# A decoder trunk on one core: squares taken off the output projections, memory tokens in smaller pieces, matmuls issued long pair then short pair

## The chip, the core and the metric

The kernel runs on one core of a Trainium2 chip. The metric is the device time of one execution in microseconds (us). A core has several engines that run at the same time, each with its own queue of instructions in order: TensorE (PE; its weight loads are listed apart as PEld), VectorE (DVE), ScalarE (ACT), GpSimd (POOL) and SyncE (SP), which issues the DMA transfers here. SBUF is the on-chip memory, PSUM the memory that matmuls accumulate in.

## The reference

One layer of a decoder with 256 positions and a width of 2048, in float32, then a final RMS norm:

```python
h = rms_norm(x, norm_mix[l])
z = h @ w_in[l]
...
x = x + jnp.concatenate([out_a, out_b, out_c], axis=-1) @ w_out[l]
h = rms_norm(x, norm_xattn[l])
m = rms_norm(mem, norm_mem[l])
q = (h @ xattn_wq[l]).reshape(bsz, S, X_HEADS, HEAD_DIM)
kv = (m @ xattn_wkv[l]).reshape(bsz, n_mem, 2, X_HEADS, HEAD_DIM)
...
x = x + o @ xattn_wo[l]
h = rms_norm(x, norm_mlp[l])
x = x + jnp.square(jax.nn.relu(h @ w_up[l])) @ w_down[l]
```

out_a is a gated MLP with a layer norm, out_b a dilated attention, out_c a sparse attention; o is a cross attention over 256 memory tokens (mem). Each RMS norm needs the sum of squares of a row of 2048.

## The kernel before

**Precision.** Every large product is made in three parts. An activation or a weight tile is split into a high part (ScalarE copies it to fp32r, L82 or with a gain L87) and a low part (VectorE subtracts the high part from the source, L83 or L88). The product is high x high + low activation x high weight + high activation x low weight. For weights the parts are called wh and wl, the source raw. A weight tile of 512 KB comes by DMA into one of five raw buffers; wh and wl have three buffers each.

**Products with weights on the left.** `gemm_t` makes a product that comes out transposed (features on partitions, positions along the row). It takes four chunks of 512 rows; each chunk is one weight tile, one wh and one wl, and `products_t` issues its 16 matmuls: for each of four row blocks kk and two feature blocks f a long matmul (`main`, 512 columns: high and low activation side by side against wh, L158) and a short one (`low`, 256 columns: high activation against wl, L162). The two f have accumulators in different PSUM banks. `low` goes first except in the first row block of a product. `gemm_t` serves the products k, cq, bk, bq, u, wo (output projection), mk, xq and up; the first product, cmp, calls `products_t` itself. `gemm` (L204, all long: dn, mv, bv, v) and `gemm_t1` (L147, all short: xo) are other helpers.

**Stages.** cmp and k first, then the sparse and the dilated attention, the gating branch (v with a layer norm into zu, then u0 and u1, then the matmuls psv with the gating weights into mix0), eight output projections wo0 to wo7 (each makes 256 of the 2048 features, from the four mix tiles in the order 2, 3, 1, 0), memory keys mk, queries xq, scores, memory values mv, eight products xo, then four times eight products up and four products dn.

**Squares and memory tokens.** After each output projection and each xo, `add_residual` adds the product to the residual xres on VectorE (L565), scales and splits it for the next product (tiles h, L87 and L88), and calls `add_squares`: ScalarE squares (L101), and POOL adds into ssq (L103), or VectorE at the start of the kernel. The memory tokens are loaded, scaled and split (tiles mT) and squared (ssqm) behind the projections wo2 to wo5, 512 KB at a time, through the same five raw buffers. `mean_eps` sums the squares over partitions (half of it on POOL) and TensorE adds them up (pss).

**Order.** The program is written in this order, but the build schedules it against a model of the engines: on each engine the instructions stand in the order that this scheduler chose, which can pull work forward over other work whose inputs come later. What runs is that order, not the text's.

Of the kernel before, what the change touches and what calls it, by code (L numbers as in the profile page):

```python
# [8 lines left out]
F32 = mybir.dt.float32  # L9
F32R = mybir.dt.float32r  # L10
AF = mybir.ActivationFunctionType
ALU = mybir.AluOpType
# [3 lines left out]
P = 128  # L16
S = 256
# [20 lines left out]
def trunk_kernel(ctx: ExitStack, tc: tile.TileContext, a, out):  # L38
# [6 lines left out]
    nc = tc.nc  # L45
# [21 lines left out]
    def slot(tag, name, dtype=F32R):  # L67
        t = ap.tile([P, 4, 2, S], F32R, tag=tag, name=name)
        return t if dtype == F32R else f32(t)
# [6 lines left out]
    def load_raw(src, n=1024):  # L76
        t = wp.tile([P, 1024], F32, tag="raw", bufs=5, name="raw")
        loads.append(nc.sync.dma_start(t[:, :n], src))
        return t[:, :n]
# [5 lines left out]
    def split_scaled(hi, lo, src, g):  # L85

        nc.scalar.activation(hi, src, AF.Copy, scale=g)  # L87
        nc.vector.scalar_tensor_tensor(lo, src, g, f32(hi), op0=ALU.mult, op1=ALU.subtract)  # L88
# [6 lines left out]
            split_scaled(t[:, k % 4, 0, :], t[:, k % 4, 1, :], src[:, i, :], gT[:, gi, k:k + 1])  # L95


    def add_squares(ssq, src, first, add=None):

        sq = ssq if first else sp.tile([P, 2, S], F32, tag="sq", name="sq")  # L100
        nc.scalar.activation(sq, src, AF.Square)  # L101
        if not first:
            (add or nc.gpsimd).tensor_tensor(ssq, ssq, sq, op=ALU.add)  # L103

    def mean_eps(ssq, name):

# [44 lines left out]
    def products_t(acc, x, wh, wl, first, last):  # L151

        for kk in range(4):
            for f in range(2):
                fs = slice(f * P, (f + 1) * P)

                def main(start, stop):
                    nc.tensor.matmul(acc[:, f].rearrange("p a s -> p (a s)"), wh[:, kk, fs],  # L158
                                     x[:, kk].rearrange("p a s -> p (a s)"), start=start, stop=stop)

                def low():
                    nc.tensor.matmul(acc[:, f, 0, :], wl[:, kk, fs], x[:, kk, 0, :], start=False, stop=False)  # L162

                if first and kk == 0:
                    main(True, False)
                    low()
                else:
                    low()
                    main(False, last and kk == 3)

    def gemm_t(lhs, wsrc, name, order=None, between=None):

        acc = pacc.tile([P, 2, 2, S], F32, tag="acc", name=name)
        order = order or list(range(len(lhs)))
        for n, b in enumerate(order):
            wh, wl = (w.rearrange("p (k n) -> p k n", k=4) for w in split_w(load_raw(wsrc[b])))
            products_t(acc, lhs[b], wh, wl, n == 0, n == len(order) - 1)
            if between is not None:
                next(between, None)
        return acc  # L180
# [97 lines left out]
    def squares():  # L278

        for m, acc in enumerate(cmps):  # L280
            join(acc, "cmp", kraw[:, 2 * m:2 * m + 2, :])
        for b in range(4):
            for n in (2 * b, 2 * b + 1):
                add_squares(ssq, xres[:, 2 * n:2 * n + 2, :], n == 0, add=nc.vector)
            yield

    acc_k0 = gemm_t(hx, a["w_t"][KV], "k0", between=squares())
# [249 lines left out]
    nc.vector.tensor_tensor(zv, zv, lng[:, 0:1, :].to_broadcast([P, 2, NB]), op=ALU.mult)  # L537
    nc.vector.tensor_tensor(zv, zv, lng[:, 1:2, :].to_broadcast([P, 2, NB]), op=ALU.add)

    for m in range(2):  # L540
        acc = gemm_t(hx, a["w_t"][UU + m], f"u{m}")
        j = join(acc, "u")
        nc.vector.tensor_tensor(j, j, rxb[:, None, :].to_broadcast([P, 2, S]), op=ALU.mult)
        nc.scalar.activation(uT[:, 2 * m:2 * m + 2, :], j, AF.Gelu_apprx_tanh)
# [14 lines left out]
            split(mix[0][:, g, 0, :], mix[0][:, g, 1, :], uT[:, g, :])  # L559


    def add_residual(acc, parts, n, ssq, act, gi):
        xs = xres[:, 2 * n:2 * n + 2, :]
        for i in range(parts):
            nc.vector.tensor_tensor(xs, acc[:, :, i, :], xs, op=ALU.add)  # L565
        put_act(act, 2 * n, xs, gi)
        add_squares(ssq, xs, n == 0)


    ssq = sp.tile([P, 2, S], F32, tag="ssq", name="ssq2")  # L570
    ssqm = sp.tile([P, 2, S], F32, tag="ssq", name="ssqm")
    h2 = new_act("hA", "h2")
    mT = []
    for n in range(8):
        acc = gemm_t(mix, a["w_out"][n], f"wo{n}", order=[2, 3, 1, 0])
        add_residual(acc, 2, n, ssq, h2, 1)
        if n >= 2 and n < 6:
            j = n - 2
            mT.append(slot("hC", f"mT{j}"))
            raw = load_raw(a["memT"][j]).rearrange("p (k s) -> p k s", k=4)  # L580
            for kk in range(4):
                split_scaled(mT[j][:, kk, 0, :], mT[j][:, kk, 1, :], raw[:, kk, :], gT[:, 2, 4 * j + kk:4 * j + kk + 1])
            for i in range(2):
                add_squares(ssqm, raw[:, 2 * i:2 * i + 2, :], j == 0 and i == 0)
    rm = rstd(mean_eps(ssqm, "mm"), "rm")
    rmb = along_free(rm, "rmb")

# [1 line left out]
    xk, xq = slot("hB", "xk"), slot("hB", "xq")  # L589
    xv = slot("hB", "xv", F32).rearrange("p k a s -> p (k a s)")[:, :1024].rearrange("p (t n) -> p t n", t=2)  # L590
    px = slot("hB", "px", F32)
    for m in range(2):
        acc = gemm_t(mT, a["w_mk"][m], f"mk{m}")
        join_split(acc, xk[:, 2 * m:2 * m + 2, 0, :], xk[:, 2 * m:2 * m + 2, 1, :], "mk", rmb)
    for m in range(2):
        acc = gemm_t(h2, a["w_q"][m], f"xq{m}")
# [26 lines left out]
    for h in range(4):  # L623
# [8 lines left out]
        for mb in range(2):  # L632
            nc.tensor.matmul(o, xv[:, mb, h * HD:(h + 1) * HD], pT[:, mb, :], start=(mb == 0), stop=(mb == 1))
        split(oT[:, h, 0, :], oT[:, h, 1, :], o)
    ssq = sp.tile([P, 2, S], F32, tag="ssq", name="ssq3")
    h3 = new_act("hB", "h3")
    for n in range(8):
        add_residual(gemm_t1(oT, a["w_xo"][n][0], f"xo{n}"), 1, n, ssq, h3, 3)


    gfin = slot("hA", "gfin", F32).rearrange("p k a s -> p (k a s)")
# [4 lines left out]
    for q in range(4):  # L646
        hid = new_act("hC", f"hid{q}")
        for c in range(8):
            acc = gemm_t(h3, a["w_up"][8 * q + c], f"up{q}{c}")
            z = join(acc, "up")  # L650
            nc.vector.scalar_tensor_tensor(z, z, 0.0, z, op0=ALU.max, op1=ALU.mult)  # L651
            ht = hid[c // 2][:, 2 * (c % 2):2 * (c % 2) + 2]
            split(ht[:, :, 0, :], ht[:, :, 1, :], z)
            if q == 0:
                if c == 0:
                    r3 = mean_eps(ssq, "m3")
                    nc.vector.reciprocal(r3, r3)
                t, n = c % 2, c // 2
                ps = pmisc.tile([P, 4, P], F32, tag="tr", name="trx")
                for i in range(4):  # L660
                    nc.tensor.transpose(ps[:, i, :], xres[:, 4 * n + i, t * P:(t + 1) * P], ident)
                nc.scalar.activation(xt[t][:, n * NB:(n + 1) * NB], ps.rearrange("p i s -> p (i s)"), AF.Copy)
        for n in range(4):
            ns = slice(n * NB, (n + 1) * NB)
            final = q == 3 and n == 3
            acc = gemm(hid, a["w_down"][4 * q + n], 2, NB, f"dn{q}{n}", hold=4 if final else 0)
            for t in range(2):
                xs = xt[t][:, ns]
                nc.vector.scalar_tensor_tensor(xs, acc[t], r3[:, t:t + 1], xs, op0=ALU.mult, op1=ALU.add)  # L669
                if q == 3:  # L670
                    j = sp.tile([P, NB], F32, tag="sq", name="sqf")
                    nc.scalar.activation(j, xs, AF.Square, accum_out=ssqf[:, t, n:n + 1])
                    if not final:
                        nc.vector.tensor_tensor(xs, xs, gfin[:, ns], op=ALU.mult)
                if q == 3 and n == 2:

                    nc.vector.tensor_reduce(sf[:, t:t + 1], ssqf[:, t, :3], axis=AX.X, op=ALU.add)
                    nc.vector.tensor_scalar(sf[:, t:t + 1], sf[:, t:t + 1], 1.0 / D, EPS, op0=ALU.mult, op1=ALU.add)  # L678
                if final:
                    s_ = sf[:, t:t + 1]  # L680
                    nc.vector.scalar_tensor_tensor(s_, ssqf[:, t, 3:4], 1.0 / D, s_, op0=ALU.mult, op1=ALU.add)
# [104 lines left out]
```

## Time and profile before

| | |
|---|---|
| median of 3 runs (lowest to highest) | 1205.95 us (1204.63 to 1206.29) |
| the profiled execution's own time | 1206.72 us |
| its span in the trace | 1204.7 us |
| granted TensorE clock, mean | 0.999 |
| longest group of TensorE waits | 4.3 us, at the start |
| DMA | 224.24 MB, 186 GB/s over the span |

The profile is of one execution. Busy time is the time in which an engine runs an instruction; a share says nothing of which engine sets the end. The chain of work follows the last instruction back to what released it, step by step, so its steps on TensorE are the distance from one matmul to the next. The rows of waits give total us, number and longest. Windows give the busy time of every engine between two times. The rows of groups give the busy us and the mean ns of one, and the length of one matmul there holds its latency too, so that neighbours overlap.

### The profile page before, as it was taken

Reading aid. Unit: us, or ns where it says so; the run is one execution under the profiler, and the core shown is the slowest. Engines: PE = TensorE matmul, PEld = TensorE weight load, DVE = VectorE, ACT = ScalarE, POOL = GpSimd, SP = SyncE. Lnnn points to the kernel's source line nnn. Section 1 sums busy time; section 2 is a strip of 40 time slices with the busy share of each in tenths; the row PEclk is TensorE's granted clock in tenths of the full one; section 3 lists DMA queues with packets and bytes.
Section 4 is the critical chain, followed back from the end, with each engine's and each line's share of the span. In section 5 each row is a group of like instructions: output and inputs, shape, how many; then the busy total and the mean of one; then the engine's idle time right before and its main releaser. Section 6 shows DMA issues by size and latency. Waiting matters only on the chain.

```text
span 1204.7 us, 16460 instructions
## 1 busy us (share of the span) xinstructions
PE 1183.8 (98%) x6450; PEld 1018.5 (85%) x6450; DVE 743.3 (62%) x911; ACT 592.2 (49%) x808; POOL 42.9 (4%) x39
## 2 busy tenths in 40 slices
PE   7999999999989999999999999999999999999996
PEld 6898888888878889888888888888888888888885
DVE  7775786666886667756544565545566545556554
ACT  7564555454665466544433444433444333444443
POOL 0000000000123001100000000000000000000000
PEclk9999999999999999999999999999999999999999
DMA  8675434545566554555665555555555555555653
GB/s 288 213 265 184 138 123 136 182 158 181 178 218 202 188 171 163 177 190 188 190 197 193 186 183 192 192 192 193 190 180 190 193 194 193 190 188 181 196 188 105
DMA packets 65385, 224.24 MB, mean 186 GB/s; under 512 B 7963, under 2 KB 9499, under 8 KB 65179
## 3 DMA queue, kind: packets, MB, share of 16 engines
q1 hardware_dynamic: 65307, 223.19, 57.0%
q8 instruction: 50, 0.82, 0.3%
q14 instruction: 28, 0.23, 0.1%
HBM read 221.06 MB, written 2.10 MB: 185 GB/s over the span
## 4 chain that ended last, share of the span: by engine, by line
PE 92%; DVE 3%; DMA 2%; issue 1%; ACT 1%; SPq 0%; ACTq 0%; POOLq 0%; POOL 0%; DVEq 0%
PE dn L204 27%; PE up L158 20%; PE up L162 10%; PE wo L158 3%; PE cq L158 2%; PE xo L147 2%; PE bv L204 2%; PE v L204 2%; PE mv L204 2%; PE wo L162 2%; DVE wl L83 1%; PE cq L162 1%; PE xq L158 1%; PE u L158 1%; PE bk L158 1%
## 5 line engine op out<-in xcount | busy, mean ns | idle before, releaser
L83 DVE TENSOR_TENSOR wl<-raw,wh 128x1024 fp32r<-128x1024 f32 (+3 forms) x414 | 500.6, 1212 | 345.9 <-ACT wh L82 344.1
L82 ACT ACTIVATE wh<-raw 128x1024 fp32r<-128x1024 f32 (+3 forms) x414 | 428.8, 1038 | 445.0 <-PE dn L204 185.5
L158 PE MATMUL up<-h,wh 128*128 128x512 f32 x1024 | 359.3, 398 | 0.0
L204 PE MATMUL dn<-wh,hid 128*128 128x512 f32 x992 | 306.1, 389 | 0.0
L162 PE MATMUL up<-h,wl 128*128 128x256 f32 x1024 | 282.4, 281 | 0.0
L158 PEld LDWEIGHTS up<-h,wh 128*128 128x128 f32 x1024 | 190.6, 188 | 44.2
L204 PEld LDWEIGHTS dn<-wh,hid 128*128 128x128 f32 x992 | 186.2, 188 | 38.7
L162 PEld LDWEIGHTS up<-h,wl 128*128 128x128 f32 x1024 | 193.3, 189 | 2.7
L204 PE MATMUL dn<-wl,hid 128*128 128x512 f32 x496 | 193.2, 389 | 0.6 <-DVE sf L678 0.6
L204 PEld LDWEIGHTS dn<-wl,hid 128*128 128x128 f32 x496 | 93.1, 188 | 20.3 <-DVE wl L83 1.2
L158 PE MATMUL wo<-mix,wh 128*128 128x512 f32 x256 | 89.4, 395 | 0.7 <-ACT wh L82 0.7
L162 PE MATMUL wo<-mix,wl 128*128 128x256 f32 x256 | 70.5, 281 | 3.1 <-DVE wl L83 3.1
L158 PEld LDWEIGHTS wo<-mix,wh 128*128 128x128 f32 x256 | 47.6, 188 | 11.2 <-ACT wh L82 1.1
L162 PEld LDWEIGHTS wo<-mix,wl 128*128 128x128 f32 x256 | 48.2, 188 | 4.9 <-DVE wl L83 4.2
L185 ACT ACTIVATE half<-up 128x512 f32<-128x512 f32 x32 | 19.1, 597 | 56.7 <-PE up L158 56.7
L158 PE MATMUL cq<-hx,wh 128*128 128x512 f32 x128 | 45.5, 397 | 0.0
L187 DVE TENSOR_TENSOR half<-up,half 128x512 f32<-128x512 f32 x32 | 22.1, 692 | 35.5 <-ACT half L185 35.5
L162 PE MATMUL cq<-hx,wl 128*128 128x256 f32 x128 | 35.3, 281 | 0.0
L669 DVE SCALAR_TENSOR_TENSOR xt<-dn,m,xt 128x512 f32<-128x512 f32 x32 | 22.6, 747 | 14.4 <-PE dn L204 14.4
L158 PE MATMUL cmp<-hx,wh 128*128 128x512 f32 x64 | 25.1, 431 | 4.3 <-ACT wh L82 4.3
L82 ACT ACTIVATE hid<-half 128x512 fp32r<-128x512 f32 x32 | 20.2, 632 | 17.1 <-DVE half L651 17.1
L158 PEld LDWEIGHTS cq<-hx,wh 128*128 128x128 f32 x128 | 23.9, 188 | 5.1
(281 smaller groups left out, 1376.5 us busy)
## 6 DMA issues: line engine op xcount, KB each, us to landing
raw<-in_w_up SPq DMA_DIRECT2D x128, 512.0 KB, 4.3
raw<-in_w_down SPq DMA_DIRECT2D x128, 512.0 KB, 4.4
raw<-in_w_t SPq DMA_DIRECT2D x52, 512.0 KB, 3.7
raw<-in_w_out SPq DMA_DIRECT2D x32, 512.0 KB, 4.0
raw<-in_w_bv SPq DMA_DIRECT2D x8, 512.0 KB, 3.7
raw<-in_w_v SPq DMA_DIRECT2D x8, 512.0 KB, 3.6
raw<-in_w_mk SPq DMA_DIRECT2D x8, 512.0 KB, 4.2
raw<-in_w_q SPq DMA_DIRECT2D x8, 512.0 KB, 3.9
```

The costliest lines, as they stand in the source:

```text
L82: nc.scalar.activation(hi, src, AF.Copy)
L83: nc.vector.tensor_tensor(lo, src, f32(hi), op=ALU.subtract)
L147: nc.tensor.matmul(acc[:, f, 0, :], w[:, kk, fs], x[:, kk, l, :], start=(kk == 0 and j == 0), stop=(kk == 3 and j == 2))
L158: nc.tensor.matmul(acc[:, f].rearrange("p a s -> p (a s)"), wh[:, kk, fs], x[:, kk].rearrange("p a s -> p (a s)"), start=start, stop=stop)
L162: nc.tensor.matmul(acc[:, f, 0, :], wl[:, kk, fs], x[:, kk, 0, :], start=False, stop=False)
L185: nc.scalar.activation(lo, acc[:, :, 1, :], AF.Copy)
L187: nc.vector.tensor_tensor(d, acc[:, :, 0, :], lo, op=ALU.add)
L204: nc.tensor.matmul(acc[t][:, :n], lhs[k // 4][:, k % 4, l, ts], w[:, kk, :], start=(k == 0 and j == 0), stop=(k == KD - 1 and j == 2))
L669: nc.vector.scalar_tensor_tensor(xs, acc[t], r3[:, t:t + 1], xs, op0=ALU.mult, op1=ALU.add)
```

## The change

Three edits. First, `products_t` issues the two long matmuls of a row block and then its two short ones, except in the last row block of a product, where the short ones go first. Second, `add_squares` always adds on VectorE, and the squares of the residual are written as a generator, `stream_squares`: for the norm before the cross attention between the chunks of mk, for the norm before the MLP in the first eight up products (the reciprocal of its mean is made in the eighth, not in the first). Third, the memory tokens are a generator of eight pieces of 256 KB, each with a buffer of a ring that the attention used before (tag "s", two buffers), written between the chunks of u1 and behind the first output projections.

```diff
-    def add_squares(ssq, src, first, add=None):
+    def add_squares(ssq, src, first):
         sq = ssq if first else sp.tile([P, 2, S], F32, tag="sq", name="sq")
         nc.scalar.activation(sq, src, AF.Square)
         if not first:
-            (add or nc.gpsimd).tensor_tensor(ssq, ssq, sq, op=ALU.add)
+            nc.vector.tensor_tensor(ssq, ssq, sq, op=ALU.add)
+
+    def stream_squares(ssq):
+        for n in range(8):
+            add_squares(ssq, xres[:, 2 * n:2 * n + 2, :], n == 0)
+            yield
...
         for kk in range(4):
-            for f in range(2):
...
-                if first and kk == 0:
-                    main(True, False)
-                    low()
-                else:
-                    low()
-                    main(False, last and kk == 3)
+            xk = x[:, kk].rearrange("p a s -> p (a s)")
+            def mains(start, stop):
+                for f in range(2):
+                    nc.tensor.matmul(acc[:, f].rearrange("p a s -> p (a s)"), wh[:, kk, f * P:(f + 1) * P], xk,
+                                     start=start, stop=stop)
+            def lows():
+                for f in range(2):
+                    nc.tensor.matmul(acc[:, f, 0, :], wl[:, kk, f * P:(f + 1) * P], x[:, kk, 0, :],
+                                     start=False, stop=False)
+            if last and kk == 3:
+                lows()
+                mains(False, True)
+            else:
+                mains(first and kk == 0, False)
+                lows()
...
+    def memory():
+        for j in range(4):
+            mT.append(slot("hC", f"mT{j}"))
+            src = a["memT"][j].rearrange("p (k s) -> p k s", k=4)
+            for i in range(2):
+                raw = sp.tile([P, 768], F32, tag="s", name="mraw")[:, :2 * S].rearrange("p (k s) -> p k s", k=2)
+                loads.append(nc.sync.dma_start(raw, src[:, 2 * i:2 * i + 2, :]))
+                for k in range(2):
+                    kk = 2 * i + k
+                    split_scaled(mT[j][:, kk, 0, :], mT[j][:, kk, 1, :], raw[:, k, :],
+                                 gT[:, 2, 4 * j + kk:4 * j + kk + 1])
+                add_squares(ssqm, raw, j == 0 and i == 0)
+                yield
+    mgen = memory()
     for m in range(2):
-        acc = gemm_t(hx, a["w_t"][UU + m], f"u{m}")
+        acc = gemm_t(hx, a["w_t"][UU + m], f"u{m}", between=mgen if m else None)
...
     for n in range(8):
         acc = gemm_t(mix, a["w_out"][n], f"wo{n}", order=[2, 3, 1, 0])
-        add_residual(acc, 2, n, ssq, h2, 1)
-        if n >= 2 and n < 6:
...
+        add_residual(acc, 2, n, h2, 1)
+        next(mgen, None)
...
     for m in range(2):
-        acc = gemm_t(mT, a["w_mk"][m], f"mk{m}")
+        acc = gemm_t(mT, a["w_mk"][m], f"mk{m}", between=sgen)
...
             if q == 0:
-                if c == 0:
+                next(sgen)
+                if c == 7:
                     r3 = mean_eps(ssq, "m3")
```

What the scheduler makes of it is seen in the rows of its order (line, operation, output and inputs, columns, "x2" for two alike). TensorE before, at the start of the first up product behind a dn product (h30 is the first chunk of the activations):

```order
L204 MATMUL dn03_6010<-wh_6139,hid03_4753 128x512
L158 MATMUL up10_6161<-h30_4430,wh_6164 128x512
L162 MATMUL up10_6161<-h30_4430,wl_6165 128x256
L158 MATMUL up10_6161<-h30_4430,wh_6164 128x512
L162 MATMUL up10_6161<-h30_4430,wl_6165 128x256 x2
L158 MATMUL up10_6161<-h30_4430,wh_6164 128x512
```

And of the change, at the same place:

```order
L212 MATMUL dn03_6018<-wh_6147,hid03_4739 128x512
L164 MATMUL up10_6169<-h30_4437,wh_6172 128x512 x2
L169 MATMUL up10_6169<-h30_4437,wl_6173 128x256 x2
L164 MATMUL up10_6169<-h30_4437,wh_6172 128x512 x2
L169 MATMUL up10_6169<-h30_4437,wl_6173 128x256 x2
```

The widths change after every second matmul instead of after nearly every one, and the first two matmuls of a chunk need wh alone.

VectorE before, in the output projections wo3 and wo4, where the memory tokens (mT2, mT3) stand:

```order
L565 TENSOR_TENSOR xres_79<-wo3_3220,xres_79 128x512 x2
L83 TENSOR_TENSOR wl_3383<-raw_3380,wh_3382 128x1024
L88 SCALAR_TENSOR_TENSOR mT2_3433<-raw_3434,gT_73,mT2_3433 128x256 x4
L88 SCALAR_TENSOR_TENSOR h21_2910<-xres_79,gT_73,h21_2910 128x256 x2
L83 TENSOR_TENSOR wl_3405<-raw_3402,wh_3404 128x1024
```

VectorE of the change, in the output projections after wo0 (ssq is the sum of squares of the residual):

```order
L592 TENSOR_TENSOR xres<-wo_3157,xres 128x512 x2
L83 TENSOR_TENSOR wl<-raw,wh 128x1024
L88 SCALAR_TENSOR_TENSOR h_2945<-xres,gT,h_2945 128x256 x2
L103 TENSOR_TENSOR ssq_3767<-ssq_3767,sq 128x512
L83 TENSOR_TENSOR wl<-raw,wh 128x1024 x3
```

The memory tokens are gone from there. The adds of the residual's squares still stand there, though they are written between the chunks of mk: the scheduler pulled them forward, and they are VectorE's now.

VectorE of the change at the seam of u0 and u1, where the memory pieces (mT1) stand among the layer norm's steps (zu) and the wl of u1 (wl_2787, wl_2817, wl_2848):

```order
L103 TENSOR_TENSOR ssqm_2688<-ssqm_2688,sq_2842 128x512
L545 TENSOR_TENSOR zu_2520<-zu_2520,lng_2519 128x1024
L83 TENSOR_TENSOR wl_2787<-raw_2784,wh_2786 128x1024
L88 SCALAR_TENSOR_TENSOR mT1_2867<-mraw_2868,gT_73,mT1_2867 128x256 x2
L103 TENSOR_TENSOR ssqm_2688<-ssqm_2688,sq_2874 128x512
L546 TENSOR_TENSOR zu_2520<-zu_2520,lng_2519 128x1024
L83 TENSOR_TENSOR wl_2817<-raw_2814,wh_2816 128x1024
L88 SCALAR_TENSOR_TENSOR mT1_2867<-mraw_2899,gT_73,mT1_2867 128x256 x2
L195 TENSOR_TENSOR half_2778<-u0_2689,half_2778 128x512
L103 TENSOR_TENSOR ssqm_2688<-ssqm_2688,sq_2905 128x512
L83 TENSOR_TENSOR wl_2848<-raw_2845,wh_2847 128x1024
```

Before, the same stretch of VectorE's queue held the zu steps, the wl and half alone.

More of the change, by code (lines that the diff above doesn't have):

```diff
@@ L153, in products_t @@
         for kk in range(4):
-            for f in range(2):
[L155 to L162, printed above, removed]
-                if first and kk == 0:
-                    main(True, False)
-                    low()
-                else:
-                    low()
-                    main(False, last and kk == 3)
+            xk = x[:, kk].rearrange("p a s -> p (a s)")
[13 more added lines that the diff above has]
+                lows()
     def gemm_t(lhs, wsrc, name, order=None, between=None):
@@ L283, in squares @@
             for n in (2 * b, 2 * b + 1):
-                add_squares(ssq, xres[:, 2 * n:2 * n + 2, :], n == 0, add=nc.vector)
+                add_squares(ssq, xres[:, 2 * n:2 * n + 2, :], n == 0)
             yield
@@ L538, in trunk_kernel @@
     nc.vector.tensor_tensor(zv, zv, lng[:, 1:2, :].to_broadcast([P, 2, NB]), op=ALU.add)
+    ssqm = sp.tile([P, 2, S], F32, tag="ssq", name="ssqm")
+    mT = []
+    def memory():
[12 more added lines that the diff above has]
+    mgen = memory()
     for m in range(2):
-        acc = gemm_t(hx, a["w_t"][UU + m], f"u{m}")
+        acc = gemm_t(hx, a["w_t"][UU + m], f"u{m}", between=mgen if m else None)
         j = join(acc, "u")
@@ L559, in trunk_kernel, with add_residual @@
             split(mix[0][:, g, 0, :], mix[0][:, g, 1, :], uT[:, g, :])
-    def add_residual(acc, parts, n, ssq, act, gi):
+    def add_residual(acc, parts, n, act, gi):
         xs = xres[:, 2 * n:2 * n + 2, :]
@@ L566, in add_residual @@
         put_act(act, 2 * n, xs, gi)
-        add_squares(ssq, xs, n == 0)
-    ssq = sp.tile([P, 2, S], F32, tag="ssq", name="ssq2")
-    ssqm = sp.tile([P, 2, S], F32, tag="ssq", name="ssqm")
     h2 = new_act("hA", "h2")
-    mT = []
     for n in range(8):
         acc = gemm_t(mix, a["w_out"][n], f"wo{n}", order=[2, 3, 1, 0])
-        add_residual(acc, 2, n, ssq, h2, 1)
-        if n >= 2 and n < 6:
[L578 to L584, printed above, removed]
+        add_residual(acc, 2, n, h2, 1)
+        next(mgen, None)
     rm = rstd(mean_eps(ssqm, "mm"), "rm")
@@ L591, in trunk_kernel @@
     px = slot("hB", "px", F32)
+    ssq = sp.tile([P, 2, S], F32, tag="ssq", name="ssq2")
+    sgen = stream_squares(ssq)
     for m in range(2):
-        acc = gemm_t(mT, a["w_mk"][m], f"mk{m}")
+        acc = gemm_t(mT, a["w_mk"][m], f"mk{m}", between=sgen)
         join_split(acc, xk[:, 2 * m:2 * m + 2, 0, :], xk[:, 2 * m:2 * m + 2, 1, :], "mk", rmb)
@@ L634, in trunk_kernel @@
         split(oT[:, h, 0, :], oT[:, h, 1, :], o)
-    ssq = sp.tile([P, 2, S], F32, tag="ssq", name="ssq3")
     h3 = new_act("hB", "h3")
     for n in range(8):
-        add_residual(gemm_t1(oT, a["w_xo"][n][0], f"xo{n}"), 1, n, ssq, h3, 3)
+        add_residual(gemm_t1(oT, a["w_xo"][n][0], f"xo{n}"), 1, n, h3, 3)
+    ssq = sp.tile([P, 2, S], F32, tag="ssq", name="ssq3")
+    sgen = stream_squares(ssq)
     gfin = slot("hA", "gfin", F32).rearrange("p k a s -> p (k a s)")
```

## The prediction

> **What bounds the kernel now.** I read the page first: the busy shares, then the chain of work that ended last.
>
> ```profile
> span 1204.7 us, 16460 instructions
> PE 1183.8 (98%) x6450; PEld 1018.5 (85%) x6450; DVE 743.3 (62%) x911; ACT 592.2 (49%) x808; POOL 42.9 (4%) x39
> PE 92%; DVE 3%; DMA 2%; issue 1%; ACT 1%; SPq 0%; ACTq 0%; POOLq 0%; POOL 0%; DVEq 0%
> ```
>
> TensorE is busy for 98% of the span and is 92% of the chain. Another engine's work only counts where TensorE stands still for it, so there are two ways to gain: shorten TensorE's own steps, or remove one of its few waits. The profiled execution took 1206.7 us (its span and 2.0 us around it), 0.8 us above the median of the three runs, 1205.95. I work from 1206.7. A measurement of this kernel can tell about 0.2%, or 2.4 us, from no change.
>
> Next the waits of TensorE alone (total us, times, longest), and the windows of the output-projection stage (length, busy time of PE, PEld, DVE, ACT, POOL):
>
> ```profile
> PE cmp L158 <- ACT wh L82: 4.3, 1, 4.3
> PE wo L162 <- DVE wl L83: 3.1, 3, 1.6
> PE cmp L162 <- DVE wl L83: 2.3, 3, 1.6
> PE wo L158 <- ACT wh L82: 0.7, 1, 0.7
> ...
> 325.00:336.00 11.00, 10.27 (x59) 8.64 (x59) 9.62 (x9) 5.28 (x7) 2.81 (x2) 1.00 0.69 230
> 336.00:349.00 13.00, 11.49 (x65) 9.56 (x64) 10.45 (x12) 9.14 (x16) 4.28 (x3) 1.00 0.54 185
> 349.00:360.00 11.00, 9.38 (x54) 7.98 (x54) 10.09 (x12) 6.83 (x11) 4.27 (x3) 1.00 0.65 207
> ```
>
> Apart from the start (cmp), TensorE waits in one place: the middle of the output projections (wo), where the memory tokens are scaled and the squares are added. It loses 0.73 + 1.51 + 1.62 = 3.9 us in these three windows, and VectorE is 85% full there (30.2 of 35 us). The waits are for wl, VectorE's product.
>
> Then TensorE's own steps. The chain in order of time gives the step from each matmul to the next (start us, us). "up L158" is a long matmul (512 columns), "up L162" a short one (256); the first three rows are every third long one:
>
> ```profile
> 705.34 0.24 PE up L158
> ...
> 706.40 0.24 PE up L158
> ...
> 707.46 0.24 PE up L158
> ...
> 707.82 0.46 PE up L158 x2
> ...
> 708.63 0.24 PE up L162 x2
> ...
> 719.11 0.46 PE up L158 x2
> ...
> 298.08 0.23 PE wo L158
> ...
> 299.12 0.23 PE wo L158
> ...
> 471.56 2.86 PE xo L147 x24
> ...
> 575.87 87.04 PE dn L204 x384
> ```
>
> In the up stage three long-short pairs take 1.06 us, **0.353 us a pair**. In a stretch of wo the same pairs take 1.04 us for three (298.08 to 299.12), 0.347. Matmuls of one width are the floor: long ones in dn 87.04/384 = 0.2267, short ones in xo 2.86/24 = 0.1192, together 0.346. So alternation costs up to 0.007 us a pair over the floor, and TensorE falls into either rhythm. From 707.82 to 719.11 is one up product, 32 pairs in 11.29 us, 0.3527 a pair.
>
> **Part 1: long pair, then short pair.** In 4 matmuls the old order has four changes of width, the new has two. No stretch of the trace runs L L S S steadily, so I bound a pair. Below: 0.346, the floor. Above: 0.353, nothing gained. The nearest rows stand at the seam between two up products, where two long ones take 0.46 and two short ones 0.24: 0.350 a pair, but these sit inside the slow rhythm. I take **0.348**, halfway between that row and the floor. The up stage has
>
> ```profile
> L158 PE MATMUL up<-h,wh 128*128 128x512 f32 x1024 | 359.3, 398 | 0.0
> ```
>
> 1024 pairs: 1024 x 0.0047 = 4.8 us (at 0.350 2.8, at 0.346 6.9, at 0.353 nothing). The other products of this helper (wo, cq, and cmp, k, bk, bq, u, mk, xq) have 256 + 128 + 7 x 64 = 832 pairs. Those of wo are partly in the fast rhythm already, and I found no steadily slow stretch as long as up's, so I give them 1.0 us, between 0 and 832 x 0.007 = 5.8. **Term: -5.8 us**, bounds 0 and -12.7. The dn and xo products use other helpers and keep their time.
>
> By the section "Back-to-back issue gap" of TensorE: Matmul & The Clock Gate, in the Trainium skill, a warm matmul follows the last after N/2.4 + 2.5 ns, whatever stands before it. That gives 215.8 + 109.2 = 325 ns a pair in either order, so this term would be nothing, and the sum 1203.4; the trace's 353 and 347 ns for the same pair already differ from it and from each other.
>
> In the new order a chunk (four row blocks of one weight tile) starts with two long matmuls that need wh alone, so wl may come 0.46 us later than now. In the cmp stage (2.3 us of waits for wl) this helps only if the low part of hx is there too, and VectorE makes that behind the wl products in its queue. I count nothing there, between -0.9 (four long matmuls ahead) and +0.9.
>
> **Part 2: squares leave POOL and the memory tokens leave the middle of wo.** Here is why VectorE fell behind there (start, length, engine, tiles):
>
> ```profile
> 338.35 0.88 DVE L88 SCALAR_TENSOR_TENSOR h<-xres,gT,h 128x256 fp32r<-128x256 f32 x2
> 340.74 5.55 DVE L83 TENSOR_TENSOR wl<-raw,wh 128x1024 fp32r<-128x1024 f32 x3 [1.50 <-ACT wh L82]
> 346.21 1.41 DVE L565 TENSOR_TENSOR xres<-wo,xres 128x512 f32<-128x512 f32 x2
> 347.88 1.23 DVE L83 TENSOR_TENSOR wl<-raw,wh 128x1024 fp32r<-128x1024 f32 x1 [0.26 <-ACT wh L82]
> 349.02 1.92 DVE L88 SCALAR_TENSOR_TENSOR h<-xres,gT,h 128x256 fp32r<-128x256 f32 x2
> ...
> 349.24 1.41 POOL L103 TENSOR_TENSOR ssq<-ssq,sq 128x512 f32<-128x512 f32 x1 [5.17 <-ACT sq L101]
> ...
> 346.78 1.06 ACT L82 ACTIVATE wh<-raw 128x1024 fp32r<-128x1024 f32 x1 [3.66 <-DMA raw<-in_w_out]
> ...
> L103 POOL TENSOR_TENSOR ssq<-ssq,sq x14: 1297/1460/1577, 314.6 to 488.9; 128x512 f32<-128x512 f32 x14
> ...
> L103 DVE TENSOR_TENSOR ssq<-ssq,sq x7: 680/684/693, 9.1 to 26.3; 128x512 f32<-128x512 f32 x7
> ```
>
> Two scalings take VectorE 0.88 us with POOL quiet and 1.92 us when a POOL add of 1.41 runs beside them; three wl take 5.55 instead of 3 x 1.23. So a POOL add costs VectorE about 1.0 us although it isn't VectorE's. The same add on VectorE costs 0.68 (the last row: min, median and longest ns, as in the start stage). Moving 21 of them is no added load where VectorE was being held up: 14 x 0.68 = 9.5 us in wo and its neighbourhood against some 14 us of holding. What remains for VectorE in one wo product is 4 x 1.23 (wl) + 1.41 (xres) + 0.88 (h) + 0.68 (add) = 7.9 us against 32 x 0.349 = 11.2 of TensorE, which covers it. The ACT row shows another late part: a w_out load that landed 3.66 us late, since the memory loads took buffers of the same raw ring; they now have buffers of their own. **Term: -3.9 us**, bounds 0 (the waits remain) and -4.6 (if the start-to-start steps are a little longer than the idle time shows).
>
> What is late next is the u products, where eight pieces of memory now stand. The work before the change there, and the lead of VectorE:
>
> ```profile
> 258.00:274.20 16.20, 16.20 (x90) 13.98 (x89) 10.18 (x13) 9.95 (x17) 0.70 (x1) 1.00 0.49 160
> 274.20:290.00 15.80, 15.80 (x98) 14.08 (x98) 10.29 (x15) 7.51 (x11) 0.00 (x0) 1.00 0.50 168
> 290.00:302.00 12.00, 12.00 (x71) 10.47 (x70) 7.81 (x13) 6.05 (x9) 0.00 (x0) 1.00 0.55 176
> ...
> 269.96 1.22 DVE L83 TENSOR_TENSOR wl<-raw,wh 128x1024 fp32r<-128x1024 f32 x1
> 273.74 0.46 PE u L158 x2
> ```
>
> VectorE has 28.3 us of work in these 44; 16 scalings of 0.44 (7.0 us) and 7 adds of 0.68 (4.8) make it 40.1, or 91%. The wl of u1's first chunk is ready at 271.2, 2.5 us ahead of the seam at 273.7. VectorE's queue is in order: behind each piece (0.88 + 0.68 = 1.56 us) stand the next wl, and behind the four scalings of the first two pieces stands the end of the layer norm, on which the gating matmuls (psv) wait. ScalarE gets the same pieces. I take **+0.6 us** for one late wl out of eight, between 0 and 11.8 (all the added work, none covered). The loads come in order on SP: the third to eighth piece wait there for two buffers, and w_out loads stand behind them. These are needed no sooner than about 283 us, and the pieces ahead of them free their buffers from about 267 on; I count nothing, and 3.7 (such a late load, as in the row above) once if that cover goes.
>
> The squares of the xo and mk stages: on POOL they held VectorE, on VectorE they cost 0.68 each, and TensorE's only wait in xo was 0.2 us. Nothing, between -0.2 and +0.7.
>
> **Sum:** 1206.7 - 5.8 - 3.9 + 0.6 = **1197.6 us**.
>
> **Rivals.**
> *The order of widths doesn't matter* (slow rhythm kept, or a new one of the same length). For it: one kernel shows both rhythms with the same instructions, so the order alone doesn't set them; the eight matmuls from 707.82 hold a seam and are no faster than their neighbours as a whole. Against: both widths alone run at the floor. Only part 2 is left: 1206.7 - 3.9 + 0.6 = 1203.4. The Trainium skill's rule above is this rival.
> *Slower: VectorE becomes the bound in the u products.* If its lead of 2.5 us at u1 is used up by the first two pieces (2 x 1.56 = 3.1 us and the layer norm between), every later piece falls on TensorE: 8 x 0.88 + 7 x 0.68 = 11.8 us, 1206.7 + 11.8 - 3.9 - 5.8 = 1208.8. It decides from the point where wl ends after the chunk's second long matmul. For it: 91% full, an in-order queue. Against: 0.46 us of new slack per chunk, and wh and wl have three buffers each, so that a lead can be rebuilt.
> *The squares and pieces stay where they hurt.* The scheduler pulls work forward: in the new order the adds of wo still stand between wo's wl products, only on VectorE, and the last four scalings stand in wo's first product. If VectorE's queue rather than POOL caused the waits, 3.9 us stay: 1206.7 - 5.8 = 1200.9. Against: the 1.92 beside 0.88.
>
> **How the numbers follow.** Forecast 0.55 (1191.5 to 1201), order of no effect 0.20 (about 1203.4), pieces stay 0.13 (about 1201), slower 0.12 (about 1209). The predicted time is the forecast's. The range reaches from 1191.5 (0.346 in up with 2 us from the others, waits gone: 1206.7 - 8.9 - 4.6 = 1193.2, and 1.7 for a better start and more of the other products) to 1204, which takes in the second and third cases and leaves out the slower one and some 0.05 below. Faster by over 0.2% means below 1203.5: forecast, third case and about half of the second, 0.78; within 0.2% 0.12; slower 0.10.
>
> **What would show it.** Up product seams 11.1 us apart instead of 11.29 show part 1 right; 11.29 shows it wrong, and more than 11.3 shows a worse rhythm. Wo windows with TensorE full and the pair of h scalings at 0.88 throughout show part 2. A row of u or wo matmuls waiting for wl, or psv waiting for zu, between 262 and 300 us shows the price. I'd be wrong above all if the L L S S rhythm settles at 0.353, or if the layer norm's end slips.

## The result, and the profile after

| | before | after |
|---|---|---|
| median (lowest to highest) | 1205.95 us (1204.63 to 1206.29) | 1197.03 us (1196.85 to 1197.58) |
| the profiled execution's own time | 1206.72 us | 1197.19 us |
| its span in the trace | 1204.7 us | 1195.4 us |

The ratio of after to before is 0.9929, with a 95% interval of 0.9912 to 0.9946: the change gains 8.9 us, or 0.7%. The forecast was 1197.6, reached from the profiled execution's 1206.72; the profiled execution of after took 1197.19.

The page of after, the busy shares and the chain:

```profile
PE 1178.5 (99%) x6450; PEld 1016.5 (85%) x6450; DVE 738.8 (62%) x932; ACT 589.6 (49%) x808; POOL 13.1 (1%) x18
...
PE 96%; ACT 1%; issue 1%; DVE 1%; DMA 1%; SPq 0%; ACTq 0%; POOLq 0%; POOL 0%
```

TensorE executes as many matmuls as before. GpSimd (POOL) has 21 instructions fewer (18 instead of 39), VectorE (DVE) 21 more, and yet VectorE's busy time went down by 4.5 us (743.3 to 738.8). TensorE's share of the chain rose from 92% to 96%.

The waits of TensorE in after (what it waits for: us in total, times, longest):

```profile
PE cmp L164 <- ACT wh L82: 6.0, 5, 4.5
PE ox L651 <- DVE oT L83: 0.7, 1, 0.7
PE dn L212 <- DVE sf L698: 0.6, 1, 0.6
PE dn L212 <- DVE wl L83: 0.5, 1, 0.5
PE xo L153 <- DVE xres L592: 0.2, 1, 0.2
```

Both wo rows are gone. No row for u or psv took their place. At the start the waits for wl became waits for wh.

The windows of after, first the u stage and then the output projections (length, busy time and count of PE, PEld, DVE, ACT, POOL, then clock, DMA share, GB/s):

```profile
258.00:274.20 16.20, 16.20 (x93) 14.16 (x92) 12.89 (x21) 14.84 (x29) 0.70 (x1) 1.00 0.52 179
274.20:290.00 15.80, 15.80 (x98) 14.03 (x97) 15.55 (x25) 10.49 (x17) 0.19 (x1) 1.00 0.72 236
290.00:302.00 12.00, 12.00 (x73) 10.55 (x72) 10.39 (x21) 7.42 (x12) 2.54 (x2) 1.00 0.61 200
...
325.00:336.00 11.00, 11.00 (x65) 9.59 (x64) 7.51 (x9) 5.56 (x7) 0.00 (x0) 1.00 0.54 188
336.00:349.00 13.00, 13.00 (x77) 11.37 (x76) 8.09 (x10) 6.62 (x8) 0.00 (x0) 1.00 0.56 184
349.00:360.00 11.00, 11.00 (x65) 9.63 (x64) 7.34 (x10) 5.56 (x7) 0.00 (x0) 1.00 0.59 185
```

In wo TensorE is now full in all three windows (35.0 of 35 us, 31.1 before), with VectorE at 22.9 us instead of 30.2. In the u stage VectorE has 38.8 us of work in 44, and 15.55 in 15.8 in the middle one, and still TensorE shows no idle time there.

Two tiles on VectorE, the scaling into h and the add of the squares (count, then shortest, median and longest in ns, first and last start in us); the first row is of before, the two others of after:

```profile
L88 DVE SCALAR_TENSOR_TENSOR h<-xres,gT,h x14: 475/479/1525, 303.7 to 372.9; 128x256 fp32r<-128x256 f32 x14
```

```profile
L88 DVE SCALAR_TENSOR_TENSOR h<-xres,gT,h x14: 477/479/480, 307.4 to 367.1; 128x256 fp32r<-128x256 f32 x14
...
L103 DVE TENSOR_TENSOR ssq<-ssq,sq x21: 680/684/693, 9.3 to 481.2; 128x512 f32<-128x512 f32 x21
```

The longest scaling fell from 1525 to 480 ns, and the add on VectorE takes 680 to 693 ns wherever it stands.

The chain in time of after, in the up stage (start us, us; L164 is the long matmul, L169 the short one), the seam of two products, and the same seam three products later:

```profile
699.92 0.93 PE up L164 x4
700.85 0.23 PE up L169 x2
701.08 0.47 PE up L164 x2
...
733.42 0.93 PE up L164 x4
```

The seams are 33.50/3 = 11.17 us apart instead of 11.29: 0.349 us a pair instead of 0.3527. The prediction had named 11.1 as the sign that part 1 is right.

**Where the time came from.** The first matmuls of four stages, TensorE's timeline, before and then after (start us, us):

```profile
33.85 0.40 PE L158 MATMUL k<-hx,wh 128*128 128x512 f32 x1
...
261.20 0.39 PE L158 MATMUL u<-hx,wh 128*128 128x512 f32 x1
...
381.79 0.47 PE L158 MATMUL mk<-mT,wh 128*128 128x512 f32 x1
...
483.91 0.48 PE L158 MATMUL up<-h,wh 128*128 128x512 f32 x1
```

```profile
32.40 0.62 PE L164 MATMUL k<-hx,wh 128*128 128x512 f32 x2
...
259.56 0.62 PE L164 MATMUL u<-hx,wh 128*128 128x512 f32 x2
...
375.23 0.62 PE L164 MATMUL mk<-mT,wh 128*128 128x512 f32 x2
...
477.84 0.71 PE L164 MATMUL up<-h,wh 128*128 128x512 f32 x2
```

| stretch | gain, us |
|---|---|
| start, up to k | 33.85 - 32.40 = 1.45 |
| k to u | 227.35 - 227.16 = 0.2 |
| u and wo | 120.59 - 115.67 = 4.9 |
| mk to xo | 102.12 - 102.61 = -0.5 |
| up and dn, the rest of the span's 9.3 | 3.2 |

The half microsecond lost from mk to xo is in part work that moved: 24 transposes of the residual (trx) are recorded there instead of 18, and 32 in the whole kernel in both cases; the others run in up. Each value of this table is a difference of two single executions; the section on e8 shows how much the start alone scatters.

### The profile page after: what moved, and what is told of

Same layout as the page of the kernel before. It is cut to its first block, busy times and chain, and to the rows that moved or that the text cites. A ratio compares the mean times of both kernels' runs of the same rounds, so it can differ in the third digit from the quotient of the medians.

```text
span 1195.4 us, 16480 instructions
## 1 busy us (share of the span) xinstructions
PE 1178.5 (99%) x6450; PEld 1016.5 (85%) x6450; DVE 738.8 (62%) x932; ACT 589.6 (49%) x808; POOL 13.1 (1%) x18
## 4 chain that ended last, share of the span: by engine, by line
PE 96%; ACT 1%; issue 1%; DVE 1%; DMA 1%; SPq 0%; ACTq 0%; POOLq 0%; POOL 0%
PE dn L212 28%; PE up L164 20%; PE up L169 10%; PE wo L164 5%; PE cq L164 3%; PE wo L169 2%; PE xo L153 2%; PE v L212 2%; PE bv L212 2%; PE mv L212 2%; PE k L164 1%; PE cq L169 1%; PE bq L164 1%; PE mk L164 1%; PE u L164 1%; PE xq L164 1%
## 5 line engine op out<-in xcount | busy, mean ns | idle before, releaser
L83 DVE TENSOR_TENSOR wl<-raw,wh 128x1024 fp32r<-128x1024 f32 (+3 forms) x414 | 495.6, 1200 | 332.3 <-ACT wh L82 331.0
L164 PE MATMUL up<-h,wh 128*128 128x512 f32 x1024 | 317.2, 395 | 0.0
L169 PEld LDWEIGHTS up<-h,wl 128*128 128x128 f32 x1024 | 187.8, 188 | 42.0
L169 PE MATMUL up<-h,wl 128*128 128x256 f32 x1024 | 197.1, 279 | 0.0
L164 PEld LDWEIGHTS up<-h,wh 128*128 128x128 f32 x1024 | 158.4, 189 | 2.7
L164 PE MATMUL wo<-mix,wh 128*128 128x512 f32 x256 | 79.2, 396 | 0.0
L169 PEld LDWEIGHTS wo<-mix,wl 128*128 128x128 f32 x256 | 46.6, 188 | 10.2
L169 PE MATMUL wo<-mix,wl 128*128 128x256 f32 x256 | 49.1, 279 | 0.0
L164 PE MATMUL cq<-hx,wh 128*128 128x512 f32 x128 | 40.5, 396 | 0.0
L164 PEld LDWEIGHTS wo<-mix,wh 128*128 128x128 f32 x256 | 39.7, 189 | 0.8
L169 PEld LDWEIGHTS cq<-hx,wl 128*128 128x128 f32 x128 | 23.6, 188 | 5.1
L164 PE MATMUL cmp<-hx,wh 128*128 128x512 f32 x64 | 21.5, 435 | 6.0 <-ACT wh L82 6.0
L169 PE MATMUL cq<-hx,wl 128*128 128x256 f32 x128 | 25.7, 280 | 0.0
```

The costliest lines, as they stand in the source:

```text
L83: nc.vector.tensor_tensor(lo, src, f32(hi), op=ALU.subtract)
L169: nc.tensor.matmul(acc[:, f, 0, :], wl[:, kk, f * P:(f + 1) * P], x[:, kk, 0, :], start=False, stop=False)
```

## The experiments

The two parts of the change could each have brought all of the gain, part of it, or the same part twice. The theory: the rhythm of widths is worth about 5 us in its own right, and GpSimd's adds cause the waits in wo. The rivals: the order works through the bank that a matmul writes to, or through the slack it gives to wl; and what counts in wo is where the memory tokens stand. The kernel before, measured again beside them, took 1205.76 to 1205.91 (medians).

| run | median us (lowest to highest) | ratio, 95% | up pair, ns | TensorE waits in wo, us |
|---|---|---|---|---|
| before | 1205.95 (1204.63 to 1206.29) | | 352.2 | 3.8 |
| after | 1197.03 (1196.85 to 1197.58) | 0.9929, 0.9912 to 0.9946 | 348.8 | none |
| e1_pair_only | 1199.11 (1197.83 to 1201.22) | 0.9944, 0.9931 to 0.9956 | 348.9 | 0.8 |
| e2_rest_only | 1202.15 (1201.69 to 1202.56) | 0.9966, 0.9952 to 0.9979 | 352.5 | none |
| e3_dve_adds_only | 1202.15 (1201.98 to 1203.41) | 0.9968, 0.9956 to 0.9981 | 352.5 | none |
| e4_pieces_only | 1204.93 (1203.83 to 1205.32) | 0.9988, 0.9979 to 0.9997 | 352.2 | none (1.7 in u) |
| e5_alternate_banks | 1203.61 (1203.09 to 1204.81) | 0.9981, 0.9972 to 0.9990 | 352.9 | none |
| e6_pairs_one_bank | 1197.29 (1197.07 to 1197.81) | 0.9926, 0.9910 to 0.9941 | 348.7 | none |
| e7_eight_eight | 1200.97 (1200.06 to 1201.48) | 0.9955, 0.9941 to 0.9968 | 348.6 | 0.2 (2.2 in k) |
| e9_pair_and_dve_adds | 1197.32 (1196.25 to 1198.03) | 0.9925, 0.9913 to 0.9938 | 348.9 | none |
| e8_cmp_old_order | 1198.58 (1197.86 to 1198.88) | 0.9939, 0.9926 to 0.9951 | 348.8 | none (3.8 in cmp and k) |
| e10_short_pair_first | 1201.76 (1200.80 to 1202.52) | 0.9967, 0.9955 to 0.9979 | 348.9 | 3.2 |

The pair is the mean distance from the start of a long matmul to the start of the next matmul, and the same of a short one, added, over the up stage; steps across a matmul that the trace misses are left out.

### The two parts apart

**e1_pair_only** is the kernel before with the new `products_t`, and nothing else of the change.

```diff
+            if last and kk == 3:
+                lows()
+                mains(False, True)
+            else:
+                mains(first and kk == 0, False)
+                lows()
```

> Only the long-pair-short-pair order in products_t, on the kernel before. Theory (the parts add up, and pairing is worth the difference of rhythm plus a better start): up products 11.16 us apart instead of 11.29 (0.3488 us a pair instead of 0.3527), cmp ends 1.4 us earlier, the output projections still lose 3.5 to 4.6 us to wl; about 1201 us. Rival (the new order's later need for wl is what ended the waits in wo): the waits in wo fall under 1.5 us and the time comes near 1198.

**e2_rest_only** is after with the old `products_t` (the edit against after).

```diff
-            else:
-                mains(first and kk == 0, False)
-                lows()
...
+                else:
+                    low()
+                    main(False, last and kk == 3)
```

> Everything but the new order of matmuls: squares added on VectorE, memory tokens in eight pieces from u1 on, products_t as before. Theory: the waits in wo are gone, none comes up in the u products, up stays at 11.29 us a product, the start is as before; 1201.4 us. Rival (the new order's slack for wl is needed): waits for wl of 1 us or more in u1 or wo, and 1202.5 us or more.

The order alone gained 6.8 us, the rest alone 3.8. Together that would be 10.6, and the change gains 8.9: the parts overlap. The waits of e1 show where:

```profile
PE wo L163 <- DVE wl L83: 0.6, 1, 0.6
...
PE wo L158 <- ACT wh L82: 0.2, 1, 0.2
```

With the memory tokens and GpSimd's adds still in the middle of wo, 0.8 us of the 3.8 is left. The new order removed most of these waits by itself, which the theory had not expected; it had also expected cmp to end 1.4 us earlier, and k, the stage behind it, started 0.8 us earlier (33.07 instead of 33.85).

### What ends the waits in wo

**e3_dve_adds_only** is the kernel before with one expression changed.

```diff
-            (add or nc.gpsimd).tensor_tensor(ssq, ssq, sq, op=ALU.add)
+            nc.vector.tensor_tensor(ssq, ssq, sq, op=ALU.add)
```

> The kernel before with the adds of squares on VectorE, nothing moved: memory tokens stay behind wo2 to wo5 with 512 KB loads in the raw ring. Theory (POOL's adds held VectorE up, and that made wl late): waits of TensorE in wo under 1.3 us, about 1202.5 us. Rival (the memory work itself and its loads in the raw ring): 2.6 us or more of waits remain, about 1204.7 us or more.

**e4_pieces_only** has the other half of that part: memory pieces and moved squares as in after, old `products_t`, adds on GpSimd (the edit against after; the old `products_t` is not shown).

```diff
-            nc.vector.tensor_tensor(ssq, ssq, sq, op=ALU.add)
+            (add or nc.gpsimd).tensor_tensor(ssq, ssq, sq, op=ALU.add)
```

> Memory tokens in pieces from u1 on and squares written between the chunks of mk and up as in the change, but all these adds on POOL; products_t as before. Theory (POOL's adds held VectorE up): waits of 1.5 us or more for wl or psv in u1 or wo, 1203 us or more. Rival (the place of the memory work and its buffers was the cause): under 1 us of waits, about 1201.5 us.

e3 gives the whole of e2: 1202.15 both. Its windows in wo, for the same stretches:

```profile
325.00:336.00 11.00, 11.00 (x65) 9.59 (x64) 9.69 (x15) 6.79 (x12) 0.00 (x0) 1.00 0.77 251
336.00:349.00 13.00, 13.00 (x75) 11.24 (x74) 11.73 (x19) 9.94 (x18) 0.00 (x0) 1.00 0.66 230
349.00:360.00 11.00, 10.89 (x62) 9.24 (x62) 10.65 (x16) 7.70 (x12) 0.00 (x0) 1.00 0.70 240
```

VectorE is busier than it was before (32.1 of 35 us against 30.2), with more instructions, and TensorE is full but for 0.11. So VectorE's load is not what made TensorE wait. With the adds off GpSimd the longest scaling into h is 485 ns instead of 1525, and the waits are gone although the memory tokens' work still stands there.

e4 takes the memory tokens away from wo and leaves the adds on GpSimd. Its windows in wo, for the same stretches:

```profile
325.00:336.00 11.00, 11.00 (x64) 9.55 (x63) 7.09 (x9) 5.36 (x7) 1.47 (x1) 1.00 0.58 190
336.00:349.00 13.00, 13.00 (x75) 11.31 (x74) 8.51 (x11) 7.34 (x10) 2.37 (x2) 1.00 0.53 172
349.00:360.00 11.00, 11.00 (x64) 9.54 (x63) 7.38 (x8) 5.39 (x7) 1.18 (x2) 1.00 0.58 188
```

TensorE is full here too, with GpSimd still adding the residual's squares (one add of about 1.5 us in each output projection). So the residual's adds on GpSimd don't make TensorE wait in wo by themselves either. The waits of before needed both the adds on GpSimd and the memory tokens in the same place, and taking either away is enough. Whether the tokens count by their scalings or by their own adds, which also held VectorE up, e4 doesn't tell, since both moved.

Still, e4 gains 1.0 us only, and a new wait stands in u, where the memory work now is. Its row of waits, its VectorE and its GpSimd there (start us, us):

```profile
PE u L168 <- DVE wl L83: 1.7, 2, 1.4
```

```profile
269.39 1.21 DVE L83 TENSOR_TENSOR wl<-raw,wh 128x1024 fp32r<-128x1024 f32 x1
270.53 2.31 DVE L543 TENSOR_TENSOR zu<-zu,lng 128x1024 f32<-128x1024 f32 x1
272.77 2.31 DVE L83 TENSOR_TENSOR wl<-raw,wh 128x1024 fp32r<-128x1024 f32 x1
```

```profile
270.23 1.53 POOL L103 TENSOR_TENSOR ssqm<-ssqm,sq 128x512 f32<-128x512 f32 x1 [1.04 <-ACT sq L101]
272.70 1.29 POOL L103 TENSOR_TENSOR ssqm<-ssqm,sq 128x512 f32<-128x512 f32 x1 [0.95 <-ACT sq L101]
```

A wl of 1.21 us becomes one of 2.31 where a GpSimd add of 1.29 starts 0.07 ahead of it. The holding went where the memory tokens and their adds went. The section "SBUF: two separate sides" of SBUF — State Buffer, in the Trainium skill, describes a pair of ports shared by VectorE and GpSimd that one of them holds for a whole instruction while the other waits; the 2.31 us here agree with such a lock: the add ends at 272.70 + 1.29 = 273.99, 1.21 more makes 275.20, and the wl ended at 275.08.

**e9_pair_and_dve_adds** is the kernel before with the new order and VectorE's adds; memory tokens and squares stand where they were before.

```diff
-            (add or nc.gpsimd).tensor_tensor(ssq, ssq, sq, op=ALU.add)
+            nc.vector.tensor_tensor(ssq, ssq, sq, op=ALU.add)
...
+            else:
+                mains(first and kk == 0, False)
+                lows()
```

> The kernel before with the new order of matmuls and the adds on VectorE; the memory tokens stay behind wo2 to wo5 with 512 KB loads, the squares stay beside the projections. Theory (the move of the memory tokens and squares is worth nothing of its own): 1197.0, within 0.2% of the change, no wait over 0.3 us in wo. Rival (the move is worth something once the rest is done): 1198.5 or more.

It takes 1197.32, against 1197.03 of the whole change, with ranges that overlap. Once the adds are on VectorE, moving the memory tokens and writing the squares as a stream brings nothing that these runs can tell from zero.

### What makes the pair shorter

**e5_alternate_banks** is after with widths that alternate as before, while consecutive matmuls go to the banks in another order: long of feature block u, short of v, long of v, short of u, with u and v (0 and 1) swapped in every second row block. By the edit three of four steps change the bank, not all of them as its expectation says; before it is two of four, in after every step.

```diff
+                main(kk, u)
+                low(kk, v)
+                main(kk, v)
+                low(kk, u)
```

> The changed kernel, but the widths alternate again (long, short, long, short) while each matmul goes to the other accumulator bank than the one before it, except at the first and last row block of a product. Theory (the change of width costs): 0.3527 us a pair in up, 11.29 us a product, about 1201. Rival (consecutive matmuls into one bank cost, and the new order gains because it changes banks each time): 0.3488 a pair, about 1197.

**e6_pairs_one_bank** keeps pairs of one width, but both matmuls of a pair write the same feature block.

```diff
+                    main(k0, f, start=(first and k0 == 0))
+                    main(k0 + 1, f)
+                    low(k0, f)
+                    low(k0 + 1, f)
```

> The changed kernel with long pair, short pair as before, but the pair is of two row blocks of one feature block, so that four matmuls in a row go to one bank. Theory (the change of width costs): 0.3488 us a pair in up, about 1197. Rival (one bank costs): 0.3527 a pair, about 1201.

The chain in the up stage of e5, and then of e6, from seam to seam:

```profile
692.62 0.94 PE up L160 x4
...
703.92 0.94 PE up L160 x4
```

```profile
699.55 0.93 PE up L160 x4
...
710.71 0.93 PE up L160 x4
```

e5 takes 11.30 us a product, as before the change (11.29), and e6 takes 11.16, as after it (11.17), though only one of four of its steps changes the bank. So the bank is not what counts; whether the widths alternate or come in pairs is.

e5 as a whole took 1203.61, 2.6 us over its expectation of 1201 and 6.6 over after. In up 1024 pairs at 4.1 ns make 4.2 of this. The other products lost as well: the pair in wo takes 352.8 ns in e5 and 348.9 in after.

Alternating widths are not always slow, though. In wo of before the pair took 348.9 ns on the mean, and in one stretch, in the chain, it ran close to the floor of 0.346 us:

```profile
300.75 0.23 PE wo L158
...
308.72 0.23 PE wo L158
```

These are 23 alternating pairs in 7.97 us, 0.3465 a pair, by the same code that takes 0.3527 in up. Alternating matmuls fall into a fast or a slow rhythm, and up ran mostly in the slow one; pairs of a width ran near 349 in wo and in up. What decides which rhythm alternating matmuls fall into, no run here shows.

**e7_eight_eight** is after too, and asks whether fewer changes bring more: all eight long matmuls of a chunk, then the eight short ones.

```diff
+        for kk, f in ks:
+            main(kk, f, start=(first and kk == 0), stop=(last and kk == 3))
+        if not last:
+            for kk, f in ks:
+                low(kk, f)
```

> The changed kernel with all eight long matmuls of a chunk and then its eight short ones (short ones first in the last chunk of a product): 2 changes of width in 16 matmuls instead of 8. Theory (each change of width costs about the same, 0.0039 us a pair for halving their number): 0.3469 us a pair, three quarters of the way from 0.3488 to the floor of 0.346, up products 11.10 us apart, about 1194. Rival (a rhythm that the pair order already ended, nothing left to gain): 0.3488 a pair, about 1197.

Its chain in the up stage, and its row of waits in k:

```profile
699.76 1.91 PE up L164 x16
701.67 3.65 PE up L160 x16
...
712.83 3.65 PE up L160 x16
```

```profile
PE k L164 <- DVE wl L83: 1.9, 2, 1.0
```

A product takes 712.83 - 701.67 = 11.16 us, and the pair 348.6 ns, where the expectation was close to the floor of 346. Sixteen long matmuls in a row take 3.65/16 = 0.228 each at the seam, a little over the 0.2267 of dn; the shorts take 0.119. One change in eight matmuls costs nearly as much as four in eight. So the expectation failed: the cost isn't a fixed price for each change of width. The kernel as a whole is 3.9 us slower than after. Of this 3.1 are lost by the start of cq, the next product of `gemm_t` behind k (92.31 instead of 89.20); 2.2 of these are waits for wl and wh in k. Why wl comes late there, and where the rest went, stays open.

### What the slack is worth

**e10_short_pair_first** is e1 with the short pair ahead of the long one, except in a product's first row block. The number of changes of width is that of e1; a chunk's first matmuls mostly need wl at once.

```diff
+            if first and kk == 0:
+                mains(True, False)
+                lows()
+            else:
+                lows()
+                mains(False, last and kk == 3)
```

> The kernel before with pairs, but the short pair first in every row block but a product's first: the rhythm of pairs without the slack for wl. Theory (the slack ended most of the waits in wo and gave the better start; the pairs give only the rhythm): 0.3488 us a pair in up, waits of 3 us or more for wl in wo, k starts near 33.8; about 1202.0. Rival (the pairs changed the schedule, and that ended the waits): waits in wo under 1.5 us and about 1199.

Its waits in wo, and its chain in the up stage:

```profile
PE wo L163 <- DVE wl L83: 2.7, 3, 1.7
...
PE wo L158 <- ACT wh L82: 0.5, 1, 0.5
```

```profile
705.12 0.93 PE up L158 x4
...
716.29 0.93 PE up L158 x4
```

The rhythm is that of e1, 11.17 us a product, and the waits of 3.2 us are nearly those of before. The time is 1201.76, 4.15 us under before and 2.65 over e1. So the order has two effects. The slack from having two long matmuls first is worth 2.65 us beside GpSimd's adds, 2.4 of it in these waits. The rhythm is worth some 3.5 against the mix of rhythms that before ran in: of the 4.15, 0.6 is a little less waiting in wo (3.2 instead of 3.8), and 1024 pairs in up at 0.0033 us make 3.4.

**e8_cmp_old_order** asks what the new order does at the start: after with the old order in the cmp products alone.

```diff
-            products_t(cmps[m], hx[b], wh.rearrange("p (k n) -> p k n", k=4), wl.rearrange("p (k n) -> p k n", k=4),
+            products_old(cmps[m], hx[b], wh.rearrange("p (k n) -> p k n", k=4), wl.rearrange("p (k n) -> p k n", k=4),
```

> The changed kernel with the old order of matmuls in the cmp stage alone. Theory (the start gained because the long matmuls of a row block go ahead of wl): the k product starts near 33.8 us instead of 32.4, TensorE waits for wl in cmp again (about 2 us), and the time is about 1198.4. Rival (the start gained by the other schedule of the first adds on VectorE or by chance): k starts near 32.4, about 1197.

Its waits at the start:

```profile
PE cmp L168 <- DVE wl L83: 2.9, 2, 1.7
...
PE k L189 <- DVE wl L83: 0.9, 1, 0.9
```

The time is 1198.58, 1.55 us over after. k starts at 32.87 us, earlier than the 33.8 expected, and then waits 0.9 for wl; cq, the next product of `gemm_t`, starts at 90.80 instead of 89.20. So the order in cmp brings a better start, but its size is uncertain. Over the single traces, cq starts from 89.61 to 90.80 where cmp has the old order (e4, e2, e3, before, e8; mean 90.26) and from 88.98 to 89.88 where it has the new one (e6, after, e9, e1; mean 89.39). The means are 0.9 us apart, with a scatter of about 1 us within each group.

No variant beat the change: e6 at 1197.29 and e9 at 1197.32 are within 0.03% of it and can't be told from it.

## Why the prediction was right, and where its terms were off

The forecast case came, 0.6 us from the measured median. That it came so close is in part luck: its terms were not that good, and their errors offset. The pairs brought about 2 us less than counted, the start and the u products together 1.5 to 2 more.

- **Part 1, up (predicted -4.8).** The direction held: pairs of a width leave the slow rhythm (e5 and e6). The size was off. The pair settled at 348.8 ns, not at the 348 taken halfway to the floor, and it had been 352.2 on the mean over the stage, not the 352.7 of the one product that was read. 1024 x 0.0034 = 3.5 us; up and dn together gained 3.2, and the transposes that moved ahead of them are part of this. The reason held only in part. The prediction counted changes of width, four against two in four matmuls, and e7 shows that the cost doesn't follow their number. Its own rows of wo showed alternating matmuls close to the floor (0.347), so the gain comes from up having run mostly in the slow one of two rhythms.
- **Part 1, the other products (predicted -1.0).** The u, mk, cq and xq pairs went from 349.8 to 350.8 ns down to about 349; bk, bq and wo hardly moved, and k rose from 349.9 to 351.7. That makes 0.3 to 0.5 us.
- **Part 1, the slack for wl.** The working named it for cmp only, counted nothing there, and put its bound at 0.9. It was worth something: k started 1.45 us earlier in after (32.40 against 33.85), 0.8 earlier in e1, and e8 puts it at 1.55; by the mean starts of cq it is 0.9. So nothing was too little, and whether the bound was too tight isn't settled. The new order alone ended 3.0 of wo's 3.8 us (e1), and e10 shows that the slack did it, which the prediction did not see. It matters little for the sum, because part 2 ends them as well.
- **Part 2 (predicted -3.9).** Right in size: the waits of 3.8 us ended, and the rest of the change without the order gained 3.8 (e2). u and wo together gained 4.9 us where -3.9 + 0.6 was predicted. On the cause it was right that GpSimd's adds held VectorE up and that taking them away is enough (e3). But they were not the whole of it: in e4 they stay on GpSimd in wo, the memory tokens are gone from there, and no wait is left. In the change itself the move of the tokens adds nothing, because the adds are gone too (e3 equal to e2, e9 equal to after). The late w_out load, the other suspect, did not matter: in e3 ScalarE still stands idle for 3.06 us ahead of such a load, and no row of TensorE waiting in wo is left.
- **The price in u (predicted +0.6).** Nothing. VectorE ran 15.55 of 15.8 us there, and wl still came in time, in e2 too, which has the old order and so less slack. e4 shows what would have brought the price in: the same pieces with GpSimd's adds, in the old order, 1.7 us of waits.
- **xo and mk.** Predicted nothing, up to +0.7; 0.5 was lost from mk to xo, part of it transposes that moved in.

The rivals: that the order has no effect is ruled out by e10, in which the waits nearly stay and 4.15 us go. Its argument, that the order alone doesn't set the rhythm, was right for alternating widths. The rule of the Trainium skill that the prediction sets beside it ("Back-to-back issue gap" in TensorE: Matmul & The Clock Gate) is given there for isolated matmuls, and the section says that in a stream the weight loads count too. The 325 ns a pair worked out from it are an estimate without any term for the order; 352.9 (e5) and 348.7 (e6) for the same matmuls disagree with it in size and in the order's effect. That pieces stay where they hurt fell in an instructive way: pieces that stay do not hurt once the adds are off GpSimd (e9). VectorE as the bound in u did not come about.

What stays open is why alternating matmuls fall into a slow rhythm in one place and a fast one in another, and why a pair costs the same with changes in every second matmul and in every eighth. The runs show the sizes and that the bank is not the cause.

## What to carry to other kernels

Work given to an idle engine is not free if it holds instructions of an engine that feeds the bound: look for the same operation at two durations (here 0.48 and 1.52 us) before you move load, and count what it holds, not its own time. When the engine that bounds is full, look at its steps one by one: the same matmuls can take 1% more or less in another order, or in the same order in another stage, and an order that starts with what needs the earliest operand gives the late one slack for nothing. Two parts that end the same wait don't add up; measure them apart and together.

## What the runs showed of the hardware that was not expected

- **The order of widths.** The same long and short matmul take 352.9 ns a pair alternating (e5), 348.8 in pairs (after) and 348.6 in groups of eight (e7), against 346 from dn and xo, where one width runs alone. Alternating, they can also run at 346.5 (23 pairs in wo of before).
- **GpSimd's adds.** One of 1.3 to 1.5 us lengthens an instruction of VectorE by about 1 us: wl from 1.21 to 2.31, the h scaling from 0.48 to 1.52. Moving the 21 adds onto VectorE and nothing else (e3) took its busy time from 743.3 down to 741.6 us, though the adds themselves take 0.684 each there.
- **A full engine without a price.** VectorE at 98% over 15.8 us, with in-order work that TensorE needs, cost TensorE nothing (after); at 86% with held instructions (before, wo) TensorE lost 3.9 us.
